# A layer norm's last pass split between VectorE and TensorE, and two background jobs moved in the order

## The chip, the core and the metric

The kernel runs on one core of a Trainium2 chip. The time is that of the device, in microseconds, from one execution; the figure of a kernel is the median of its runs. The profile is of one execution of its own.

A core has five engines, each with its own in-order queue: TensorE (PE in the profile, with its weight loads as PEld), VectorE (DVE), ScalarE (ACT), GpSimd (POOL) and SyncE (SP), which here only issues DMAs. An instruction that waits holds up what is queued behind it on its engine, and nothing else.

## The reference

One decoder layer over 512 tokens of width 2048, all in float32:

```
h   = x @ w_in                                   (11808 columns)
y_a = (FoX attention(q, k, v, forget gates) * silu(z)) @ w_a
y_b = (NSA attention(compressed, selected, window) * silu(z)) @ w_b
m   = sigmoid(g_a) * y_a + sigmoid(g_b) * y_b
out = layer_norm(2^(1/4) * x + m @ w_o, ln_g, ln_b)
```

The layer norm takes mean and variance over the 2048 columns of a token and gives `(z - mean) / sqrt(var + 1e-5) * g + b`. The NSA branch has a compression of keys and values: blocks of 32 tokens go through `gelu(flat @ w1) @ w2`.

## The kernel before, in words

**Splits.** Each f32 operand of a large product is split into a high part (`hi`, written by ACT as fp32r) and a rest (`lo`, written by DVE); a product is three fp32r matmuls, hi*hi, hi*lo and lo*hi (`mm3`, L106). Weights are streamed: a load into one of three buffers `wr` (L157, on SP's queue), a split into `wh` and `wl` (L97 on ACT, L98 on DVE) three units ahead of use, then the matmuls. A buffer `wr` is free for the next load when its last split is done.

**The stream and its ticks.** The program is one hand-written stream of units, most of them four k-tiles of a product. During a unit the code calls `tick()`, in the projections once per two k-tiles (6 matmuls). A tick advances every background job (a Python generator in the list `active`, in the order in which they were added, then the heads of two queues, `tq` and `sq`) to its next `yield`. So a yield is a step in the order of the program, not a wait of the chip: it sets between which matmuls an instruction stands in PE's queue, and between which splits it stands in DVE's. `drain` runs ticks until a condition holds.

**The background jobs that matter here.** When the first projection is done, `first_evac` starts three: a job with the forget gates (DVE steps L659 to L703, with a product at L679), `lefts` and `tables`.

- `lefts` (L1044) makes the left operands of four products of a Strassen-like scheme that follows (`phase_split`). It passes ten ticks, then issues one sum of two halves of x^T per tick (L1054, 16 of them, DVE), then one split per tick (16, ACT and DVE).
- `tables` loads rows of a one-hot table, makes two products with `rel` (L627), copies each out of PSUM with DVE (`tb`, L629), stores it, and then issues two transfers that spread the table in DRAM (`skew_d`, L632, 2560 KB, and `fwd_d`, L633). Its last PE step is a transposition at L635, which takes the one PSUM bank `m` that the second copy at L629 reads.
- `cmp_finish` (L799 on) ends the compression, once for keys and once for values: DVE copies the sums out of PSUM (`parts`, L805) and makes a matrix `two` (L806); two yields later PE multiplies them (L810); then follow the gelu and the second product, with yields between.
- `fox_s` and `fox_t` are the attention's two halves. `fox_s` normalizes the rows of `p` on DVE (L395, L399), `fox_t` transposes them on PE (L408).

**The last product.** `m @ w_o` is taken in four column blocks (n = 0 to 3) of 512. For n = 0 to 2 all four token tiles run together through 16 k-tiles, one tick per k-tile; afterwards `add_all` adds x with DVE (`add_z`, L1284) and takes the statistics of the block (L1285), one tile per tick. For n = 3 tiles 0 and 1 run first, while the split weights are kept; then `o_rest(2)` and `o_rest(3)` run tile 2 and tile 3 alone, 48 matmuls each, with seven ticks each. So the norm of tiles 0 and 1 is issued beside the matmuls of tiles 2 and 3, that of tile 2 beside tile 3 and after, and that of tile 3 at the end.

**The norm before.** `norm_job` adds the last block for its tiles, then goes through `norm_steps`: combine the statistics (L1296), root on ACT (L1297), reciprocal and shift on DVE (L1298, L1299). Of the four pieces of 512 columns, piece 1 is scaled on ACT (L1305) and gets g and b on POOL (L1306, L1307); the other three take two DVE passes each: `(z - mean) * g` (L1309) and `* rstd + b` (L1310). g and b are in SBUF, broadcast to all 128 partitions by DMAs that `f_open` starts at the beginning of the last product (`consts`, L1269). A piece is stored by SP's queue (L1313) when it is done.

Of the kernel before, what the change touches and what calls it, by code (L numbers as in the profile page):

```python
# [12 lines left out]
F32 = mybir.dt.float32  # L13
F32R = mybir.dt.float32r
AF = mybir.ActivationFunctionType
# [5 lines left out]
P = 128  # L21
# [42 lines left out]
def layer(ctx, tc, x, w_in, b_f, pos_k, pos_v, wk1, wk2, wv1, wv2, w_a, w_b, w_o, ln_g, ln_b, rel, onehot, out):  # L64
    nc = tc.nc

    def dram(t, off, ap):
        return bass.AP(tensor=t.tensor, offset=t.offset + off, ap=ap)
# [731 lines left out]
    def cmp_finish(kv):  # L800

        n = G * NCMP
        parts = small("parts", 2 * n, CMP_HID)
        two = small("two", 2 * n, n)
        nc.vector.tensor_copy(parts, hid[kv][:2 * n, :CMP_HID])  # L805
        nc.vector.tensor_tensor(two, ident[:2 * n, :n], ident[:2 * n, n:2 * n], op=ALU.add)  # L806
        yield
        yield
        m = bank("m", 1)
        nc.tensor.matmul(m[:n, :CMP_HID], two, parts, start=True, stop=True)  # L810
        a, u = small("ga", n, CMP_HID), small("gu", n, CMP_HID)
        nc.vector.tensor_copy(a, m[:n, :CMP_HID])
        yield
        nc.vector.tensor_tensor(u, a, a, op=ALU.mult)
        nc.vector.tensor_scalar(u, u, 0.044715, 1.0, op0=ALU.mult, op1=ALU.add)
        nc.vector.tensor_tensor(u, u, a, op=ALU.mult)
        yield
        nc.scalar.activation(u, u, AF.Tanh, scale=math.sqrt(2.0 / math.pi))
        yield
        nc.vector.tensor_scalar(a, a, 0.5, None, op0=ALU.mult)  # L820
        nc.vector.scalar_tensor_tensor(a, u, 1.0, a, op0=ALU.add, op1=ALU.mult)
        yield
        yield
        m = bank("m", 1)
        for k in range(2):
            nc.tensor.transpose(m[:, k * 64:k * 64 + n], a[:, k * P:(k + 1) * P], ident[:n, :n])
        mk = m[:, :P].rearrange("p (k c) -> p k c", k=2)[:, :, :n]
        if kv == "k":
            ht = small("ht", P, 2 * n).rearrange("p (k c) -> p k c", k=2)
            nc.vector.tensor_copy(ht, mk)  # L830
            yield
            yield
            m = bank("m", 1)
            for k in range(2):
                nc.tensor.matmul(m[:, :n], w2t[kv][:, k], ht[:, k], start=k == 0, stop=k == 1)
            for g in range(G):
                kc = pool("attn").tile([P, 2, CP], F32R, name=f"kc{g}")
                nc.vector.memset(kc[:, :, NCMP:].bitcast(F32), 0.0)
                split(kc[:, 0, :NCMP], kc[:, 1, :NCMP], m[:, g * NCMP:(g + 1) * NCMP])
                kt_["c", g] = kc  # L840
        else:

            ht = small("ht", P, 2 * G * C3).rearrange("p (k g u c) -> p k g u c", k=2, g=G, u=3)
            nc.vector.memset(ht, 0.0)
            for u in range(3):
                nc.vector.tensor_copy(ht[:, :, :, u, :NCMP], mk.rearrange("p k (g c) -> p k g c", g=G))
            yield
            yield
            m = bank("m", 1)
            for g in range(G):  # L850
                for k in range(2):
                    nc.tensor.matmul(m[:C3, g * P:(g + 1) * P], ht[:, k, g].rearrange("p u c -> p (u c)"),
                                     w2t[kv][:, k], start=k == 0, stop=k == 1)
            for g in range(G):
                vc = pool("attn").tile([C3, DH], F32R, name=f"vc{g}")
                vt["c", g] = vc
                src, low = m[:C3, g * P:(g + 1) * P], slice(2 * CP, C3)
                nc.scalar.activation(vc, src, AF.Copy)
                nc.vector.tensor_tensor(vc[low], src[low], vc[low].bitcast(F32), op=ALU.subtract)
        done.add(("cmp", kv))  # L860
        yield
        if kv == "v":
            active.append(block_bias())
# [179 lines left out]

    def lefts():  # L1044

        for _ in range(10):
            yield
        x32 = left["x"]
        t0, t1 = slice(0, S // 2), slice(S // 2, S)
# [203 lines left out]
    def f_open():  # L1253
        close_pool("o")
        fp = open_pool("fin")
        fin["res"] = fp.tile([P, 2, KR, S], F32R, name="res")
        fin["g"] = fp.tile([P, D], F32, name="lng")
        fin["b"] = fp.tile([P, D], F32, name="lnb")
        fin["eps"] = fp.tile([P, 1], F32, name="eps")
        nc.vector.memset(fin["eps"], EPS)  # L1260
        for i in range(NT):
            fin["st", i] = fp.tile([P, NC, 6], F32, name=f"st{i}")
            fin["mv", i] = fp.tile([P, 2], F32, name=f"mv{i}")
            fin["sd", i] = fp.tile([P, 3], F32, name=f"sd{i}")

        def consts():
            for c in range(NC):
                for t, src in (("g", ln_g), ("b", ln_b)):
                    nc.gpsimd.dma_start(fin[t][:, c * S:(c + 1) * S], dram(src, c * S, [[0, P], [1, S]]))  # L1269
                    for _ in range(4):  # L1270
                        yield
        active.append(consts())

    def load_z(n):
# [7 lines left out]
    def add_z(i, n, p):  # L1282
        z = fin["z", i, n]
        nc.vector.scalar_tensor_tensor(z, z, ALPHA, p, op0=ALU.mult, op1=ALU.add)  # L1284
        nc.vector.bn_stats(fin["st", i][:, n], z)  # L1285

    def add_all(n, banks):
        for i in range(NT):
            add_z(i, n, banks[i])
            yield  # L1290

    def norm_steps(i):
        mv, sd = fin["mv", i], fin["sd", i]

        def stats():
            nc.vector.bn_aggr(mv, fin["st", i])  # L1296
            nc.scalar.activation(sd[:, :1], mv[:, 1:2], AF.Sqrt, bias=fin["eps"])  # L1297
            nc.vector.reciprocal(sd[:, 1:2], sd[:, :1])  # L1298
            nc.vector.tensor_scalar(sd[:, 2:3], mv[:, :1], sd[:, 1:2], -1.0, op0=ALU.mult, op1=ALU.mult)  # L1299

        def piece(n):
            z, c = fin["z", i, n], slice(n * S, (n + 1) * S)
            g, b = fin["g"][:, c], fin["b"][:, c]
            if n == 1:
                nc.scalar.activation(z, z, AF.Identity, scale=sd[:, 1:2], bias=sd[:, 2:3])  # L1305
                nc.gpsimd.tensor_tensor(z, z, g, op=ALU.mult)  # L1306
                nc.gpsimd.tensor_tensor(z, z, b, op=ALU.add)  # L1307
            else:
                nc.vector.scalar_tensor_tensor(z, z, mv[:, :1], g, op0=ALU.subtract, op1=ALU.mult)  # L1309
                nc.vector.scalar_tensor_tensor(z, z, sd[:, 1:2], b, op0=ALU.mult, op1=ALU.add)  # L1310

        def store(n):
            nc.sync.dma_start(dram(out, i * P * D + n * S, [[D, P], [1, S]]), fin["z", i, n])  # L1313

        def steps():
            stats()
            yield
            piece(1)
            for n in (0, 2, 3):
                piece(n)  # L1320
                store(n)
                if n == 2:
                    store(1)
                yield

        return steps()

    def norm_job(tiles):
        for i, p in tiles:
# [169 lines left out]
```

## Time and profile before

| | us |
|---|---|
| runs shown | 1541.04, 1542.46, 1541.02 (median 1541.04) |
| the profiled execution | 1544.86 |
| its span, first to last instruction | 1542.8 |
| outside the span | 2.06 |
| mean granted clock of TensorE | 0.993 of full speed |

The page gives each engine's busy time and the chain of work that ended last: followed back from the last instruction, at each step to what released it. A group's row ends with its busy time, the mean of one in ns, and the idle time of the engine before it. In a timeline a row is start, length, engine, line of the code, operation, what it writes and reads, and in brackets the engine's idle time before it with what ended it. Matmuls are pipelined: the length of one is longer than the distance to the next. The clock is the share of full speed that the throttle granted TensorE.

### The profile page before, as it was taken

What the parts mean: (1) busy time and instruction counts of PE and PEld (TensorE: products, weight loads), DVE (VectorE), ACT (ScalarE), POOL (GpSimd) and SP (SyncE); (2) the same over time, 40 slices, a digit from 0 to 9 for tenths busy, and PEclk for the clock granted to TensorE, in tenths of its full rate; (3) what the DMA queues carried; (4) which work ended last, traced back from release to release, by engine and by line L of the source; (5) the groups of instructions that cost most, each with busy time, mean ns of one, the idle gap of its engine ahead of it and who ended that gap; (6) DMA issues with size and microseconds to landing.
All of it is one profiled execution on the core that took longest, in us unless ns stands there. A gap on an engine that the chain in (4) does not pass through costs nothing.

```text
span 1542.8 us, 19662 instructions
## 1 busy us (share of the span) xinstructions
PE 1503.5 (97%) x7143; PEld 1255.1 (81%) x7143; DVE 855.6 (55%) x1683; ACT 638.6 (41%) x1254; POOL 210.3 (14%) x333
## 2 busy tenths in 40 slices
PE   7999999999999999999999999999999999999995
PEld 5778787997897878888888888888888888888884
DVE  3857666666664664554445665366635444343347
ACT  6245555555563543433334444344434222222221
POOL 0102020211114632532000000000002000030003
PEclk9999999999999999999999999999999999999998
DMA  6578685877665553443333222322226343272222
GB/s 198 133 199 208 181 198 161 187 227 173 176 155 184 144 144 89 130 139 108 82 96 90 76 76 75 83 75 76 67 84 218 119 146 119 96 259 96 96 96 109
DMA packets 202241, 207.00 MB, mean 134 GB/s; under 512 B 12992, under 2 KB 153312, under 8 KB 202144
## 3 DMA queue, kind: packets, MB, share of 16 engines
q1 hardware_dynamic: 182288, 159.41, 34.8%
q0 software_dynamic: 19856, 46.34, 13.0%
q8 instruction: 56, 0.92, 0.2%
q14 instruction: 41, 0.34, 0.1%
HBM read 189.12 MB, written 20.22 MB: 136 GB/s over the span
## 4 chain that ended last, share of the span: by engine, by line
PE 87%; DVE 6%; DMA 3%; ACT 2%; issue 1%; POOL 0%; SPq 0%; ACTq 0%; DVEq 0%
PE d L106 48%; PE s L106 12%; PE pt L106 9%; PE o L106 8%; PE m L106 5%; DMA wr<-in_w_in_dram 2%; DVE wl L98 2%; PE pt L408 2%; ACT wh L97 1%; DVE om L1309 1%; PE m L112 1%; DVE om L1310 1%; PE o L112 0%; PE d L1219 0%; DVE c L977 0%
## 5 line engine op out<-in xcount | busy, mean ns | idle before, releaser
L106 PE MATMUL d<-big,wh 128*128 128x512 f32 x1792 | 570.4, 399 | 6.9 <-ACT wh L97 3.8
L98 DVE TENSOR_TENSOR wl<-wr,wh 128x512 fp32r<-128x512 f32 (+1 forms) x492 | 331.0, 681 | 379.7 <-ACT wh L97 369.8
L97 ACT ACTIVATE wh<-wr 128x512 fp32r<-128x512 f32 (+1 forms) x492 | 300.4, 619 | 394.2 <-PE d L106 126.4
L106 PEld LDWEIGHTS d<-big,wh 128*128 128x128 f32 x1792 | 325.3, 189 | 72.3 <-ACT wh L97 5.5
L106 PE MATMUL d<-big,wl 128*128 128x512 f32 x896 | 352.6, 394 | 0.1
L106 PEld LDWEIGHTS d<-big,wl 128*128 128x128 f32 x896 | 169.2, 189 | 38.4 <-DVE wl L98 0.9
L390 ACT ACTIVATE p<-p,mn 128x128 f32<-128x128 f32 (+3 forms) x96 | 54.1, 564 | 134.6 <-DVE mn L388 134.6
L98 DVE TENSOR_TENSOR wl<-s,wh 128x512 fp32r<-128x512 f32 (+1 forms) x120 | 75.2, 637 | 54.6 <-ACT wh L97 54.4
L97 ACT ACTIVATE wh<-s 128x512 fp32r<-128x512 f32 (+1 forms) x120 | 69.2, 589 | 58.6 <-DVE wl L98 32.6
L106 PE MATMUL s<-wh,T 128*128 128x512 f32 (+1 forms) x320 | 93.2, 367 | 0.0
L106 PE MATMUL o<-wh,big 128*128 128x512 f32 (+1 forms) x224 | 84.2, 376 | 2.7 <-ACT wh L97 2.7
L106 PE MATMUL m<-wh,big 128*128 128x512 f32 (+1 forms) x224 | 83.7, 374 | 0.0
L106 PE MATMUL d<-wh,big 128*128 128x512 f32 (+1 forms) x240 | 74.4, 376 | 0.0
L98 DVE TENSOR_TENSOR pT<-pt,pT 128x512 fp32r<-128x512 f32 (+1 forms) x96 | 46.6, 489 | 44.3 <-ACT pT L97 43.8
L789 POOL TENSOR_SCALAR af<-raw,posT 128x31 f32<-128x31 f32 x128 | 66.9, 545 | 0.1
L106 PEld LDWEIGHTS s<-wh,T 128*128 128x128 f32 x320 | 59.2, 188 | 7.5
L97 ACT ACTIVATE pT<-pt 128x512 fp32r<-128x512 f32 (+1 forms) x96 | 41.3, 433 | 47.4 <-PE pt L408 46.7
L106 PE MATMUL s<-wl,T 128*128 128x512 f32 (+1 forms) x160 | 58.7, 367 | 0.0
L951 POOL DMA_DIRECT2D r<-in_w_in_dram x20 | 24.2, 1209 | 199.4 <-DVE wl L98 118.6
L106 PEld LDWEIGHTS o<-wh,big 128*128 128x128 f32 x224 | 42.0, 188 | 10.6 <-ACT wh L97 4.6
L106 PEld LDWEIGHTS d<-wh,big 128*128 128x128 f32 x240 | 44.6, 188 | 7.2 <-ACT wh L97 0.4
L480 POOL DMA_DIRECT2D bt<-skew_d x8 | 4.3, 542 | 326.3 <-DVE mn L388 257.5
(276 smaller groups left out, 2400.4 us busy)
## 6 DMA issues: line engine op xcount, KB each, us to landing
wr<-in_w_in_dram SPq DMA_DIRECT2D x148, 512.0 KB, 3.7
wr<-in_w_o_dram SPq DMA_DIRECT2D x32, 512.0 KB, 3.6
wr<-in_w_in_dram SPq DMA_DIRECT2D x24, 384.0 KB, 3.8
wr<-in_w_a_dram SPq DMA_DIRECT2D x16, 512.0 KB, 3.6
om<-sig_d POOLq DMA_DIRECT2D x32, 256.0 KB, 4.8
wr<-in_w_b_dram SPq DMA_DIRECT2D x16, 512.0 KB, 3.7
r<-in_w_in_dram SPq DMA_DIRECT2D x12, 512.0 KB, 4.9
r<-in_w_in_dram POOLq DMA_DIRECT2D x12, 512.0 KB, 11.5
```

What stands on the lines that cost most here:

```text
L97: nc.scalar.activation(hi, src, AF.Copy)
L98: nc.vector.tensor_tensor(lo, src, hi.bitcast(F32), op=ALU.subtract)
L106: nc.tensor.matmul(o, u, v, start=first and n == 0, stop=last and n == 2, **kw)
L112: nc.tensor.matmul(*u, start=first and u is whole, stop=last and u is whole)
L390: nc.scalar.activation(row, row, AF.Exp, bias=it["mn"][:, i:i + 1], scale=-1.0, accum_out=it["l"][:, i:i + 1])
L408: nc.tensor.transpose(b[:, (i - j) * P:(i - j + 1) * P], pt[:, OFF[i] + j * P:OFF[i] + (j + 1) * P], ident)
L480: nc.gpsimd.dma_start(bt, dram(skew_d, h * P * RL + P - 1, [[RL - 1, P], [1, S]]))
L789: nc.gpsimd.tensor_scalar(af[:, l, g], src, posT[:, po0 + ll:po0 + ll + 1], None, op0=ALU.add)
L951: nc.gpsimd.dma_start(two(n, k), rows(jobs[j], quad[0] * kh + k - 1, quad[1]), accum_op=ALU.add)
L1309: nc.vector.scalar_tensor_tensor(z, z, mv[:, :1], g, op0=ALU.subtract, op1=ALU.mult)
L1310: nc.vector.scalar_tensor_tensor(z, z, sd[:, 1:2], b, op0=ALU.mult, op1=ALU.add)
```

## The change

Three edits.

The norm: after `add_all` has added a block for all tiles, four ticks later it multiplies each tile's block by g with DVE (`times_g`, one tile per tick); for the last block that product stands in `norm_steps`. What is then left of a piece is `z*g * rstd + (-mean*rstd * g + b)`. The bracket is made by PE in PSUM, as a product of two rows: the left operand is the column pair (-mean*rstd, 1) of `sd`, transposed by PE and copied to SBUF by ACT (`ct`, 2 x 128), the right one the rows g and b (`gb`, 2 x 2048, plain f32). One DVE pass per piece then reads the bank and is followed by the store. The steps of a tile are: statistics; transposition; pieces 0 and 1; pieces 2 and 3; each a tick apart. ACT's and POOL's work on piece 1 is gone, and so is the broadcast of b.

`lefts` passes four ticks instead of ten ahead of its first sum. `cmp_finish` passes four yields instead of two between its copies and the product.

```diff
         nc.vector.tensor_copy(parts, hid[kv][:2 * n, :CMP_HID])
         nc.vector.tensor_tensor(two, ident[:2 * n, :n], ident[:2 * n, n:2 * n], op=ALU.add)
-        yield
-        yield
+        for _ in range(4):
+            yield
         m = bank("m", 1)
...
     def lefts():
 
-        for _ in range(10):
+        for _ in range(4):
             yield
...
-        fin["b"] = fp.tile([P, D], F32, name="lnb")
+        fin["gb"] = fp.tile([2, D], F32, name="gb")
...
-            fin["sd", i] = fp.tile([P, 3], F32, name=f"sd{i}")
+            fin["sd", i] = fp.tile([P, 4], F32, name=f"sd{i}")
+            nc.vector.memset(fin["sd", i], 1.0)
+            fin["ct", i] = fp.tile([2, P], F32, name=f"ct{i}")
 
         def consts():
+            for r, src in enumerate((ln_g, ln_b)):
+                nc.gpsimd.dma_start(fin["gb"][r:r + 1], dram(src, 0, [[0, 1], [1, D]]))
             for c in range(NC):
-                for t, src in (("g", ln_g), ("b", ln_b)):
-                    nc.gpsimd.dma_start(fin[t][:, c * S:(c + 1) * S], dram(src, c * S, [[0, P], [1, S]]))
-                    for _ in range(4):
-                        yield
+                nc.gpsimd.dma_start(fin["g"][:, c * S:(c + 1) * S], dram(ln_g, c * S, [[0, P], [1, S]]))
+                for _ in range(4):
+                    yield
...
+    def times_g(i, n):
+        z = fin["z", i, n]
+        nc.vector.tensor_tensor(z, z, fin["g"][:, n * S:(n + 1) * S], op=ALU.mult)
+
     def add_all(n, banks):
         for i in range(NT):
             add_z(i, n, banks[i])
             yield
+        for _ in range(4):
+            yield
+        for i in range(NT):
+            times_g(i, n)
+            yield
 
     def norm_steps(i):
...
+        mv, sd, ct = fin["mv", i], fin["sd", i], fin["ct", i]
+        nc.vector.bn_aggr(mv, fin["st", i])
+        nc.scalar.activation(sd[:, 3:4], mv[:, 1:2], AF.Sqrt, bias=fin["eps"])
+        times_g(i, NC - 1)
+        nc.vector.reciprocal(sd[:, 2:3], sd[:, 3:4])
+        nc.vector.tensor_scalar(sd[:, :1], mv[:, :1], sd[:, 2:3], -1.0, op0=ALU.mult, op1=ALU.mult)
+        yield
+        m = bank("m", 1)
+        nc.tensor.transpose(m[:2, :P], sd[:, :2], ident)
+        nc.scalar.activation(ct, m[:2, :P], AF.Copy)
+        yield
+        for n in range(NC):
             z, c = fin["z", i, n], slice(n * S, (n + 1) * S)
...
+            b = bank(*(("pt", 2), ("pt", 2), ("o", 1))[n % 3])
+            nc.tensor.matmul(b, ct, fin["gb"][:, c], start=True, stop=True)
+            nc.vector.scalar_tensor_tensor(z, z, sd[:, 2:3], b, op0=ALU.mult, op1=ALU.add)
+            nc.sync.dma_start(dram(out, i * P * D + n * S, [[D, P], [1, S]]), z)
+            if n % 2:
                 yield
```

More of the change, by code (lines that the diff above doesn't have):

```diff
@@ L1290, in add_all @@
             yield
-    def norm_steps(i):
[L1293 to L1301, printed above, removed]
-            z, c = fin["z", i, n], slice(n * S, (n + 1) * S)
[L1303 to L1323, printed above, removed]
@@ L1324, in steps @@
                 yield
-        return steps()
     def norm_job(tiles):
```

## The prediction

> **What bounds the kernel now.** I read the page's head and its chain of work first, then busy time by stretches for the last 40 us, then the chain, the stretches and the timeline at the two other places that the change touches.
>
> ```profile
> span 1542.8 us, 19662 instructions
> ...
> PE 1503.5 (97%) x7143; PEld 1255.1 (81%) x7143; DVE 855.6 (55%) x1683; ACT 638.6 (41%) x1254; POOL 210.3 (14%) x333
> ...
> PE 87%; DVE 6%; DMA 3%; ACT 2%; issue 1%; POOL 0%; SPq 0%; ACTq 0%; DVEq 0%
> ```
>
> TensorE (PE) carries 87% of the chain: what is added to its stream is paid in full, and VectorE's (DVE's) work beside it is mostly covered. So I look for the places where PE does not set the time. The stretches of the tail (columns: stretch, length, busy time of PE, PEld, DVE, ACT and POOL, clock, DMA):
>
> ```profile
> 1502.30:1513.40 11.10, 11.10 (x50) 9.20 (x49) 10.13 (x17) 1.57 (x4) 3.27 (x2) 1.00 0.22 81
> 1513.40:1524.60 11.20, 11.20 (x50) 9.01 (x48) 10.62 (x14) 1.77 (x3) 5.12 (x4) 1.00 0.34 127
> 1524.60:1536.70 12.10, 0.09 (x1) 0.00 (x0) 11.40 (x15) 1.11 (x2) 4.65 (x3) 0.69 0.30 112
> 1536.70:1542.80 6.10, 0.00 (x0) 0.00 (x0) 0.00 (x0) 0.00 (x0) 0.00 (x0) 0.50 0.25 88
> ```
>
> From 1502.3 both engines are full: PE with the last column's tiles 2 and 3, DVE with the norm of tiles 0 and 1. PE stops at 1524.69; DVE goes on for 12 us, so the old norm is late by that much. The last 6 us are the last store and the program's end, the same in both kernels.
>
> The other places: the chain around 67 us, and stretches at both.
>
> ```profile
> 65.50 0.60 DVE x L1054
> ...
> 67.44 0.67 DVE wl L98
> ...
> 68.12 21.96 DMA wr<-in_w_in_dram
> ...
> 90.87 9.23 PE d L106 x31
> ```
>
> ```profile
> 566.90:570.30 3.40, 1.64 (x7) 1.04 (x7) 3.01 (x8) 0.81 (x2) 1.93 (x4) 0.95 0.41 120
> 570.30:573.70 3.40, 3.40 (x12) 2.74 (x11) 2.43 (x6) 1.90 (x4) 0.00 (x0) 0.54 0.68 224
> 89.04:92.45 3.41, 1.58 (x5) 1.03 (x6) 1.60 (x3) 2.26 (x5) 0.00 (x0) 0.95 0.82 250
> 92.45:95.90 3.45, 3.45 (x10) 2.65 (x10) 3.45 (x7) 3.45 (x8) 0.00 (x0) 0.55 0.46 115
> ```
>
> At 67 us DVE is the bound: it frees a weight buffer at 68.1, the load takes 22 us, and PE resumes at 90.87. At 567 us PE idles for 1.76 of 3.40 us. After both gaps the clock is at half for 3.4 us, which costs up to 1.7 us of PE work.
>
> **The change, part by part: the tail.** DVE loses one of two passes on three pieces of a tile, POOL both passes on the fourth. DVE gains one product with g per piece (three of four earlier, beside matmuls), and PE per tile one transposition and four plain f32 products of 2 rows by 512 columns.
>
> ```profile
> L1309 DVE SCALAR_TENSOR_TENSOR om<-om,mv,lng 128x512 f32<-128x512 f32 x12 | 13.0, 1085 | 0.0
> L1310 DVE SCALAR_TENSOR_TENSOR om<-om,sd,lnb 128x512 f32<-128x512 f32 x12 | 12.6, 1050 | 0.4
> ...
> L1208 DVE TENSOR_TENSOR om<-om 128x512 f32<-128x512 f32 x8 | 5.5, 692 | 0.3
> ```
>
> ```profile
> 50.39 1.02 PE L627 MATMUL m<-oh,rb 32*8 32x512 f32 x2
> 51.34 0.73 PE L106 MATMUL d<-big,wh 128*128 128x512 f32 x2
> ...
> 64.36 0.27 PE L635 MATMUL m<-ident,po 64*128 64x64 f32 x1 [0.67 <-DVE tb L629]
> 64.56 0.73 PE L106 MATMUL d<-big,wh 128*128 128x512 f32 x2
> ```
>
> ```profile
> 1481.17 21.09 PE d L106 x93
> ```
>
> DVE's 25.6 us in L1309 and L1310 become 16 passes of some 0.68 us (10.9) and, in the tail, 4 products of 0.69 (2.8). The other 12 products lie in stretches where PE carries the chain and the weights' splits run three steps ahead; with that cover gone they would cost 12 x 0.69 = 8.3 us.
>
> PE pays. No product of two rows exists before. The nearest is L627: plain f32, 512 moving columns, 32 rows; it shows as two records and holds PE from 50.39 to 51.34, 0.95 us. The other end is the kernel's own product (L106): 21.09/93 = 0.227 us. I take 0.96, by L627, since the new operands are plain f32 too. A transposition costs 0.20 (64.36 to 64.56), and I add 0.10 for its waiting check.
>
> Where these stand decides. The background steps run every second k-tile, 6 x 0.227 = 1.36 us apart, seven of them beside each of tiles 2 and 3. Tile 0 takes five; tile 1 reaches its transposition in the last step beside tile 2; its products and all of tile 2's fall beside tile 3. So 12 products and 3 transpositions stand in PE's queue ahead of tile 3's last matmul: 12 x 0.96 + 3 x 0.30 = 12.4 us. One wait comes with them: tile 2's transposition is issued 1.36 us after tile 1's last product, but DVE then has a last pass, statistics, the g product and two small steps to do, some 2.2 us. Tile 3's matmuls, queued behind it, stand still for 0.8 us. PE's end moves by 13.2, to 1537.9.
>
> Then the last tile alone, in the old timeline:
>
> ```profile
> 1527.93 0.68 DVE L1284 SCALAR_TENSOR_TENSOR om<-om,s 128x512 f32<-128x512 f32 x1
> 1528.65 0.69 DVE L1285 BATCH_NORM_STATS2 st<-om 128x6 f32<-128x512 f32 x1
> 1529.38 0.26 DVE L1296 BATCH_NORM_AGGREGATE mv<-st 128x2 f32<-128x24 f32 x1
> 1529.68 0.29 ACT L1297 ACTIVATE sd<-mv,eps 128x1 f32<-128x1 f32 x1 [7.07 <-DVE mv L1296]
> 1530.00 0.16 DVE L1298 RECIPROCAL sd<-sd 128x1 f32<-128x1 f32 x1 [0.36 <-ACT sd L1297]
> 1530.20 0.21 DVE L1299 TENSOR_SCALAR sd<-mv,sd 128x1 f32<-128x1 f32 x1
> ...
> 1535.89 0.75 DVE L1310 SCALAR_TENSOR_TENSOR om<-om,sd,lnb 128x512 f32<-128x512 f32 x1
> ```
>
> ```profile
> 584.43 0.20 ACT L97 ACTIVATE kc<-m 128x31 fp32r<-128x31 f32 x1 [4.11 <-PE m L835]
> ```
>
> Sum and statistics 0.70 + 0.68 + 0.27; the g product 0.64 (it covers the root); reciprocal and shift 0.41; transposition and copy 0.6 (the copy by L97's 0.20); four products 3.84, with the passes behind them and only the last one showing, 0.9 with its latency. That is 8.0 us, against 1536.64 - 1524.69 = 11.95 before. **Tail: 13.2 + 8.0 - 11.95 = +9.2 us.** By the ends of the product's price: +0.7 at 0.227, +11 at 1.03. PE idles for 2.8 us ahead of the last products, longer than the 1.76 us at 567, so I expect the half clock there; 3.4 us of it cost 1.7, the 2.2 us that the products fill at least 1.1, **+1.3**.
>
> Here a rule of the Trainium skill differs from the rows (TensorE: Matmul & The Clock Gate, What's actually happening): it lets the clock fall to half after a whole idle window of about 3.4 us. This trace shows the fall after stretches that were 46 and 48% busy. By the page's rule neither the new gap nor the one at 567 us would have to pay; that case is a rival below.
>
> **The sums of x^T.** Six steps earlier puts six more sums on DVE ahead of the buffer that the chain shows.
>
> ```profile
> 49.28 0.42 DVE L686 TENSOR_SCALAR fs<-fe 8x512 f32<-8x512 f32 x1 [0.70 <-ACT fe L684]
> ...
> 53.67 0.69 DVE L295 SCALAR_TENSOR_TENSOR zo<-zo,d 128x512 f32<-128x512 f32 x1 [0.20 <-ACT zo L294]
> ...
> 63.63 0.67 DVE L629 COPY tb<-m 8x512 f32<-8x512 f32 x1
> ```
>
> ```profile
> 65.22 1.13 POOL L632 DMA_DIRECT2D skew_d<-rel_d  x1
> ```
>
> A sum takes 0.60 us in the chain, so 3.6; the idle times of 0.70 and 0.20 take in 0.9. DVE is then 2.7 late and, a link of the chain, has no gap up to 68. So the table's copy (L629) comes at 66.3; PE, which waited 0.67 us for it at L635, waits 3.3; the table's spread (L632) and the weight load start 2.7 later, and PE resumes at 93.5 instead of 90.87: +2.7. Bounds: 0, if DVE's gaps took all, and 3.6; below nothing only by the rival on this load. The long wait at L635 pulls the half clock forward, into time that PE would spend waiting for the load anyway; the wait at the load shrinks to about 1.2 us and brings none: -1.7. **+1.0.** The splits of T that come earlier gain nothing: after 92.45 PE is busy throughout.
>
> **The compress step's added yields** (two more before L810).
>
> ```profile
> 568.72 0.61 PE L810 MATMUL m<-parts,two 124*62 124x256 f32 x2 [1.76 <-DVE r L395]
> ```
>
> ```profile
> 568.68 0.49 DVE L399 TENSOR_SCALAR p<-p,r 128x512 f32<-128x512 f32 x1
> ```
>
> L810 no longer stands ahead in PE's queue while DVE is late: 1.76 us go. Late next is the transposition at L408, one step on, which needs the row that L399 ends at 569.17; PE would be there at 566.96 + 1.36 = 568.3. So 0.9 of the gap stays, and the half clock goes (1.7). **-2.5**, between -0.9 (no fall of the clock to save) and -3.5 (nothing late next).
>
> The rest I cost at nothing: the memsets and the loads of g and b (two rows and one broadcast in place of two broadcasts) are issued at the start of the last product, columns ahead of their use; on POOL's queue only the loads of x stand behind them, due a column later. The weights' splits on DVE behind the g products have three steps of slack.
>
> **Sum:** 9.2 + 1.3 + 1.0 - 2.5 = +9.0 us. The profiled execution took 1544.86 us, its span 1542.8 and 2.06 around it: 1553.9 by its own time. The median of the runs shown is 3.8 lower, perhaps without the half clocks; I carry the difference over: **1550.0 us**. A difference under about 0.2% (3.1 us) can't be told from none here.
>
> **Rivals.**
> A, the cheap product: if two rows cost PE one pass, 0.227, the tail is +0.7 without a fall of the clock, and 0.7 + 1.0 - 2.5 = -0.8: 1540.2, not slower. The tail changes by 13 us per us of price, so it decides below 0.52 us a product (+3.1 in sum). L627's 0.95 speaks against it; that its rows are 32, not 2, leaves it open. Faster by 0.2% it is only with -3.5 at 567 us and nothing lost at 68.
> B, the load at 68 us no longer late: started against other traffic, the 22 us shrink and PE's gap before 90.87 (2.9 us) and its half clock go: -4.6 in place of +1.0, so +3.4: 1544.4. Against it: the table's spread and the load move together, both behind DVE.
> C, the clock neither falls in the tail nor was saved at 567 and 90: 9.2 + 2.7 - 0.9 = +11.0: 1552.0. The two half clocks in the trace speak against it; the lower median speaks for it.
> D, PE's queue waits: each transposition comes before DVE is done, with tiles 1 and 2 losing 1.5 to 2 us more: +13: 1554. DVE's free time between passes speaks against it.
>
> **How the numbers follow.** Forecast 0.54, C 0.18, D 0.10, B 0.08 (half of it within 0.2%), A 0.10 (0.04 of it faster, 0.06 within). Faster 0.04, same 0.10, slower 0.86. The range takes in B, C and the price of 1.03 and leaves out A and the far side of D: 1544.0 to 1554.5.
>
> **What would show it.** Right: two records per new product, 0.9 to 1.0 us from start to start; PE's last matmul of tile 3 some 13 us later; DVE idle between passes in the tail; the wait at L635 above 2 us; PE resuming near 93; no gap at L810, a smaller one at L408. Wrong: products at a quarter of a microsecond, or a first weight load that lands earlier than before.

## The result, and the profile after

| | before | after |
|---|---|---|
| runs, us | 1540.0 to 1542.46, median 1541.03 (4 runs) | 1554.35, 1560.1, 1563.44, 1561.65; median 1560.88 |
| ratio of after to before | | 1.0122, 95% interval 1.0089 to 1.0154 |
| the profiled execution | 1544.86 | 1554.35 |
| its span | 1542.8 | 1552.5 |
| mean granted clock of the four runs after, in their order | | 0.995, 0.989, 0.988, 0.988 |

The changed kernel is slower by 19.85 us; 9.0 were forecast, and the range ended at 1554.5. The profiled execution of the changed kernel is the fastest of its four runs and took 9.49 us more than the profiled execution of before. So there are two things to explain: 9.5 us that the profiles show, and some 6 to 9 more that the other three runs have, at a lower mean clock.

The head of the page after, with the shares of the chain of work that ended last:

```profile
span 1552.5 us, 19741 instructions
...
PE 1524.1 (98%) x7179; PEld 1259.2 (81%) x7179; DVE 851.8 (55%) x1695; ACT 634.9 (41%) x1254; POOL 193.7 (12%) x323
...
PE 89%; DVE 5%; DMA 3%; ACT 2%; issue 1%; POOL 0%; SPq 0%; ACTq 0%; DVEq 0%
```

PE's busy time grew by 20.6 us. DVE's fell by only 3.8, because the passes that went are paid back in part by the products with g. Busy time went from the engine that carried 6% of the chain to the one that carried 87% of it.

The stretches after (columns as before: stretch, length, busy time of PE, PEld, DVE, ACT and POOL, clock, DMA):

```profile
68.86:72.27 3.41, 3.41 (x10) 2.63 (x10) 3.19 (x8) 1.12 (x2) 0.95 (x2) 0.55 0.56 105
...
89.04:92.45 3.41, 3.34 (x15) 2.44 (x13) 0.00 (x0) 0.09 (x1) 0.00 (x0) 1.00 0.92 266
...
566.90:570.30 3.40, 3.40 (x16) 2.78 (x16) 1.96 (x6) 1.86 (x4) 2.23 (x5) 1.00 0.58 157
...
1502.30:1513.40 11.10, 11.10 (x40) 6.77 (x39) 5.38 (x11) 0.57 (x2) 0.00 (x0) 1.00 0.13 49
...
1536.59:1540.00 3.41, 0.88 (x4) 0.38 (x3) 2.38 (x6) 0.29 (x1) 0.00 (x0) 0.95 0.00 0
1540.00:1549.00 9.00, 7.56 (x9) 2.58 (x9) 3.08 (x5) 0.27 (x1) 0.00 (x0) 0.50 0.23 87
1549.00:1552.50 3.50, 0.00 (x0) 0.00 (x0) 0.00 (x0) 0.00 (x0) 0.00 (x0) 0.50 0.19 75
```

The gap at 567 us is gone, and PE is nearly full in the stretch ahead of 92. In the tail DVE, which was busy for 10.13 of 11.10 us from 1502.3 on, is now busy for 5.38, while PE, full as before, gets through 40 records in place of 50. The last rows hold a surprise: from 1540 to 1549 PE is busy for 7.56 of 9.00 us, in the last tile's products, and its clock stays at half all the way. (The edges of the stretches in this text lie some 0.3 us behind the changes of the clock, hence the 0.95 to 0.97 of a stretch with a fall at its end; times of a change are given by the clock itself.)

The chain of waits after, at the products beside tile 2 (start, length, what; x4 are the four records of two products):

```profile
1507.56 1.91 PE pt L1320 x4
1509.47 1.59 PE s L106 x6
1511.06 1.05 PE o L1320 x2
1512.11 0.86 PE pt L1320 x2
```

Two records per product, and four products take 1.91 + 1.05 + 0.86 = 3.82 us: 0.955 each, all of it on the chain. The timeline after, for the end:

```profile
1526.08 0.27 PE L1314 MATMUL m<-ident,sd 128*2 128x128 f32 x1 [0.27 <-DVE sd L1311]
...
1537.08 0.39 PE L106 MATMUL s<-wh,big 128*128 128x512 f32 x1
...
1540.87 3.78 PE L1320 MATMUL pt<-gb,ct 2*128 2x512 f32 x4 [0.36 <-ACT ct L1315]
...
1544.44 1.91 PE L1320 MATMUL o<-gb,ct 2*128 2x512 f32 x2
...
1546.15 1.91 PE L1320 MATMUL pt<-gb,ct 2*128 2x512 f32 x2
...
1548.10 0.75 DVE L1321 SCALAR_TENSOR_TENSOR om<-om,sd,pt 128x512 f32<-128x512 f32 x1 [0.96 <-PE pt L1320]
```

PE's last matmul of tile 3 ends at 1537.47, where it was 1524.69. The last four products start at 1540.87 and come 1.7 to 1.8 us apart, twice the distance of those above, and each pass of DVE waits 0.96 us for its product. DVE ends at 1548.85, and the span 3.65 us later; before, it was 1536.64 and 6.16. That difference of 2.5 us shows in the queue's own waits of SP, first in the kernel before and then in the one after (waiting queue, what it waited for: us in total, times, the longest):

```profile
SPq L1494 <- PEq L1494: 3.1, 2, 2.6
```

```profile
SPq L1492 <- PEq L1492: 0.7, 2, 0.5
```

PE's queue is only the last link of that wait. At the program's end each engine's queue has a `DRAIN` behind its last work, and then the queues signal one another. POOL's instructions there, before and then after (count, shortest, median and longest in ns, first and last start in us):

```profile
L1494 POOLq EVENT_SEMAPHORE  x4: 17/17/17, 1542.1 to 1542.7; - x4
L1494 POOLq DRAIN  x3: 46/93/9028, 1533.0 to 1542.6; - x3
```

```profile
L1492 POOLq DRAIN  x3: 46/98/8924, 1370.1 to 1552.2; - x3
```

Before, POOL's first `DRAIN` is issued with POOL's last product, at 1533.0, and lasts 9.03 us, to 1542.1; POOL's next step is at 1542.1, the other queues' follow it, and the span ends 0.7 us behind it. DVE had been done since 1536.64, and SP's wait for the last store ended 3.8 us ahead of the span's end. After, POOL has no piece of the norm: its `DRAIN` of 8.92 us lies at 1370, and SP's wait for the last store ends 1.3 us ahead of the end. So the end of the old program hung on POOL, not on DVE and the store.

### The profile page after: what moved, and what is told of

The parts are those of the page before. It is cut to its first block, busy times and chain, and to the rows that moved or that the text cites. A ratio compares the mean times of both kernels' runs of the same rounds, so it can differ in the third digit from the quotient of the medians.

```text
span 1552.5 us, 19741 instructions
## 1 busy us (share of the span) xinstructions
PE 1524.1 (98%) x7179; PEld 1259.2 (81%) x7179; DVE 851.8 (55%) x1695; ACT 634.9 (41%) x1254; POOL 193.7 (12%) x323
## 4 chain that ended last, share of the span: by engine, by line
PE 89%; DVE 5%; DMA 3%; ACT 2%; issue 1%; POOL 0%; SPq 0%; ACTq 0%; DVEq 0%
PE d L106 47%; PE s L106 13%; PE pt L106 9%; PE o L106 9%; PE m L106 6%; DMA wr<-in_w_in_dram 2%; DVE wl L98 2%; PE pt L408 2%; ACT wh L97 1%; PE pt L1320 1%; PE m L112 1%; PE o L112 0%; PE d L1219 0%; PE o L1320 0%; DVE x L1054 0%
## 5 line engine op out<-in xcount | busy, mean ns | idle before, releaser
L106 PEld LDWEIGHTS m<-wh,big 128*128 128x128 f32 x224 | 42.1, 188 | 6.4
```

The lines of the kernel that those rows point to most:

```text
L106: nc.tensor.matmul(o, u, v, start=first and n == 0, stop=last and n == 2, **kw)
```

## The experiments

The theory: the loss is the norm's, and lies in two places, the price of the products on a full PE, and a clock that these products let fall, by luck in some runs more than in others. The rivals: the two moved jobs cost something too; the loss is in waits in PE's queue, not in the products; the products are dear for their time alone and the clock falls for other reasons. Each ratio below is against the kernel before on the same chip, whose medians were 1539.98 to 1541.72 us over the four sets of runs.

### e1_norm_only and e2_lefts_cmp: which edit costs

The changed kernel with `lefts` and `cmp_finish` as before, and the kernel before with those two edits alone.

```diff
 # e1_norm_only, against the changed kernel; e2_lefts_cmp is the reverse, against before
-        for _ in range(4):
-            yield
+        yield
+        yield
...
-        for _ in range(4):
+        for _ in range(10):
```

> The norm edit alone; lefts and cmp_finish as before. Theory H (the two-row products count as idle for TensorE's clock, so in most runs the clock falls to half several times between 1502 and 1537 us, up to 1.7 us each): median 1555 to 1561 us, runs several us apart, the slower ones with a mean clock near 0.988. Rival F (the extra of the unprofiled runs comes from the front of the kernel, where lefts makes VectorE late): 1549 to 1552 us (1541 + 9.2 + 1.3), runs within 2 us of one another.

> The two moved jobs alone; the norm as before. Theory H: 1541 to 1545 us (+2.7 for the sums, -0.9 to -2.5 for the yields, a half clock more or less), runs within 3 us. Rival F: 1548 us or more, with runs several us apart.

Measured: the norm alone 1559.52 us (6 runs, 1555.09 to 1566.2), ratio 1.012 [1.0099, 1.0141], mean clocks 0.985 to 0.991. The two moves alone 1541.64 us (12 runs), 1.0008 [0.9998, 1.0018]. The norm carries the whole loss, and the moves together are worth nothing that can be measured.

The stretches of the first show what the profile of the changed kernel didn't hold:

```profile
1505.05:1508.46 3.41, 3.41 (x11) 1.61 (x10) 1.49 (x2) 0.00 (x0) 0.00 (x0) 0.96 0.01 5
1508.46:1511.87 3.41, 3.41 (x7) 1.62 (x6) 0.00 (x0) 0.00 (x0) 0.00 (x0) 0.50 0.42 154
1511.87:1515.29 3.42, 3.42 (x7) 1.63 (x6) 2.33 (x6) 0.29 (x1) 0.00 (x0) 0.50 0.20 78
1515.29:1518.70 3.41, 3.41 (x11) 2.49 (x10) 0.16 (x1) 0.00 (x0) 0.00 (x0) 0.54 0.19 75
1518.70:1522.11 3.41, 3.41 (x15) 2.42 (x14) 0.00 (x0) 0.27 (x1) 0.00 (x0) 1.00 0.00 0
```

And its chain, in the same place:

```profile
1505.68 1.91 PE pt L1320 x4
...
1509.92 2.00 PE o L1320 x2
1511.92 1.71 PE pt L1320 x2
```

PE is busy for all of these 17 us, and yet the clock falls to half at 1508.2, right after a stretch of which one pair of two-row products fills 1.91 us. At half clock the next pair takes 3.71 instead of 1.91 and reaches into two stretches, and the clock comes back only after 10.24 us. From tile 2's start to PE's last matmul it is 40.39 us here, against 35.64 in the changed kernel's profile, which has no such fall: 4.75 us lost. So a full PE isn't enough to hold the clock; in this trace a stretch with these products can be followed by the fall that elsewhere follows idle time. The Trainium skill (TensorE: Matmul & The Clock Gate, What's actually happening) has the clock go by whether PE is active in windows of about 3.4 us. The 3.41 us between the changes of the clock here agree; that PE is busy throughout and is slowed all the same does not.

### e3_rows128 and e8_rows32: the same products over more rows

If it is the number of rows, the same product with rows of zeros added must hold the clock at the same price. The left operand is `sdp`, padded with zero columns before it is transposed, and `gb` gets zero rows.

```diff
-        fin["gb"] = fp.tile([2, D], F32, name="gb")
+        fin["gb"] = fp.tile([P, D], F32, name="gb")
+        nc.vector.memset(fin["gb"], 0.0)
+        fin["sdp"] = fp.tile([P, P], F32, name="sdp")
+        nc.vector.memset(fin["sdp"], 0.0)
+        nc.vector.memset(fin["sdp"][:, 1:2], 1.0)
...
-        nc.tensor.transpose(m[:2, :P], sd[:, :2], ident)
-        nc.scalar.activation(ct, m[:2, :P], AF.Copy)
+        nc.tensor.transpose(m[:, :P], sdp, ident)
+        nc.scalar.activation(ct, m[:, :P], AF.Copy)
```

(e8_rows32: 32 rows in place of 128.)

> The changed kernel with the shift product taken over 128 rows, 126 of them zero, in place of 2: the same number of products, columns and passes. Theory H, with the clock going by the rows a product uses: no fall of the clock between 1502 us and the end of tile 3's matmuls in any run, runs within 3 us, median 1550 to 1555 us, mean clock 0.994 or more. If the clock goes by something else in these products (plain f32, their length, the waits around them), or the extra lies at the front: as the changed kernel, 1554 to 1563 us.

> The shift product over 32 rows, 30 of them zero, between the changed kernel's 2 (1554 to 1566 us) and 128 (1547.7 to 1551.4 us). If TensorE's clock goes by the share of rows in use, a quarter of the rows leaves half clocks between 1502 us and the end of tile 3's matmuls: 1552 to 1560 us, runs some us apart. If a block of 32 rows is enough to count as busy: 1548 to 1552 us, mean clock 0.996 or more.

Measured: 128 rows 1549.91 us (6 runs, 1547.7 to 1551.41), 1.0057 [1.0043, 1.0071], mean clocks 0.996 to 0.999; 32 rows 1552.09 us (4 runs), 1.0068 [1.0054, 1.0081], clocks 0.995 and 0.996. Both lie below the changed kernel's interval. The stretch with twelve of the products, in the run over 128 rows, and then that run's timeline at the end:

```profile
1500.00:1536.00 36.00, 34.37 (x130) 23.55 (x128) 16.98 (x32) 1.72 (x6) 0.00 (x0) 1.00 0.23 88
```

```profile
1538.21 3.68 PE L1324 MATMUL pt<-gb,ct 128*128 128x512 f32 x4 [0.37 <-ACT ct L1319]
...
1541.73 1.02 PE L1324 MATMUL o<-gb,ct 128*128 128x512 f32 x2
...
1542.59 1.02 PE L1324 MATMUL pt<-gb,ct 128*128 128x512 f32 x2
```

The first pair of the last tile is slow as in the changed kernel, behind the same idle wait. Then the clock comes back and the next two take 0.86 from start to start, where the two-row products stayed at 1.7.

Not all that e3 gains is the clock. Beside the kernel's own matmuls a pair over 128 rows is also cheaper than one over 2. Two rows of e3's timeline, with one pair between them:

```profile
1518.65 1.95 PE L106 MATMUL s<-res,big 128*128 128x512 f32 x6
...
1521.75 1.96 PE L106 MATMUL s<-res,big 128*128 128x512 f32 x6
```

Six matmuls and a pair take 3.10 us here; in the changed kernel's chain above it was 1.59 + 1.05 + 0.86 = 3.50, at full clock too. From tile 2's start to PE's last matmul it is 33.56 us in e3's profile, against 35.64: 2.1 us that aren't the clock. Why the rows matter here isn't shown. The 32 rows have no such gain, 3.50 and 35.66 us, so e8 is the cleaner test of the clock: the same work at the same price, no fall from 1502 us to the end of tile 3's matmuls in its profile, and by the two ratios (1.0122 and 1.0068) 0.54% or some 8 us less. What is left of the loss in e8, 0.68%, is in the main the time on a full PE, less what the shorter work of DVE and the shorter end of the program save. In e3 0.65% or some 10 us went, of which 2.1 are the cheaper pairs. Its 1549.9 us is the forecast's 1550.0 by coincidence: neither those pairs nor the shorter end of the program was in the forecast.

Since all added rows hold zeros, it is not their data. Over 32 rows the clock holds beside the matmuls, but in the one profile it doesn't come back in the last tile.

### e4_four_at_once: all products of a tile in one step

```diff
-            if n % 2:
-                yield
+        yield
```

> The changed kernel with all four products of a tile in one step, 3.9 us of two-row products in a row instead of two pairs. Theory H: a stretch of 3.4 us can no longer miss them, so the profile itself shows a half clock behind the products of each of tiles 0 to 2, and every run has at least three falls there; 1554 to 1562 us. Rival F: full clock in the profile from 1502 us to the end of tile 3's matmuls.

Measured: 1553.15 us (4 runs, 1551.95 to 1555.09), 1.008 [1.0063, 1.0098]. The median is below what was expected, and 7.7 us below that of the changed kernel, though the two intervals touch. Its stretches at tiles 0 and 1:

```profile
1505.13:1508.54 3.41, 3.41 (x8) 1.14 (x7) 2.24 (x3) 0.00 (x0) 0.00 (x0) 0.97 0.20 79
1508.54:1511.96 3.42, 3.42 (x9) 2.69 (x9) 1.75 (x5) 0.29 (x1) 0.00 (x0) 0.53 0.59 228
1511.96:1515.37 3.41, 3.41 (x14) 2.17 (x13) 0.00 (x0) 0.27 (x1) 0.00 (x0) 1.00 0.02 5
1515.37:1518.78 3.41, 3.41 (x10) 1.43 (x9) 2.79 (x4) 0.00 (x0) 0.00 (x0) 0.97 0.39 152
1518.78:1522.20 3.42, 3.42 (x10) 2.73 (x9) 1.62 (x4) 0.00 (x0) 0.00 (x0) 0.53 0.40 155
```

A group of four fills nearly a stretch, and behind those of tiles 0 and 1 the clock falls, but for one stretch only, in which the kernel's own matmuls stand. Behind tile 2's group it stays at 1.00, so the three falls expected were two: that group lay across two stretches, with 1.97 us of products in the first. Pairs are better spread by the eye and worse by the clock: at half clock each pair takes 3.7 us and keeps the clock down for the pair behind it. Whether a first pair makes it fall differs from run to run. The Trainium skill (TensorE: Matmul & The Clock Gate, What's actually happening) calls the windows free-running, so that a kernel's work falls into them otherwise in each execution. The changes of the clock in the changed kernel's profile agree that they keep a beat of their own: from 71.96 to 1539.69 us it is 430 times 3.413. That this is the whole reason isn't shown. Nor is it shown how much of a stretch the products must fill. Two stretches, cut here by the clock's own beat, first of e1 and then of e4, with the products alone (columns: stretch, length, busy time of PE and PEld, clock, DMA; the last product's overlap counts in):

```profile
1504.74:1508.16 3.42, 1.98 (x4) 0.66 (x4) 1.00 0.00 0
```

```profile
1525.42:1528.84 3.42, 1.97 (x5) 1.00 (x6) 1.00 0.00 0
```

The products fill the same time in both, yet the clock fell behind the first and stayed at 1.00 behind the second.

### e11_one_pass: the product at a quarter of the price

```diff
-        fin["gb"] = fp.tile([2, D], F32, name="gb")
+        fin["gb"] = fp.tile([2, D], F32R, name="gb")
...
-            fin["ct", i] = fp.tile([2, P], F32, name=f"ct{i}")
+            fin["ct", i] = fp.tile([2, P], F32R, name=f"ct{i}")
```

g and b are loaded into two rows of the buffer of g first and copied into `gb` by ACT, which rounds them.

> The changed kernel with the shift product in fp32r, one pass; it leaves out the low parts of the shift, of g and of b in that product. Two rows, as changed. If the price of the plain f32 product is the main term: products of 0.23 us in the profile and, since a pair now fills under 0.5 us of 3.4, no half clock before the end of tile 3's matmuls: 1541 to 1546 us, runs within 4 us. Rival: the norm's cost lies in its waits and its order (transposition, VectorE behind PE) more than in the product's price: 1548 us or more.

Measured: 1540.92 us (11 runs, 1540.09 to 1542.59), 1.0002 [0.9993, 1.0011]. Its timeline:

```profile
1524.52 0.50 PE L1326 MATMUL o<-gb,ct 2*128 2x512 f32 x1
1524.85 0.39 PE L1326 MATMUL pt<-gb,ct 2*128 2x512 f32 x1
```

One record a product, 0.33 us from start to start, and no half clock from 70.2 to 1534.5 us. Both parts of the loss are gone together, and the whole change then comes out at no difference: DVE's shorter tail and the shorter end of the program are worth what the transpositions, their waits and the cheap products cost. It doesn't tell the price from the clock, since it takes away both; e8 and e3 do that.

### e5_cmp_only, e6_lefts_only, e7_later_sums, e9_sums13: the moved jobs

```diff
 # e5_cmp_only against before: cmp_finish with four yields, lefts as before
-        yield
-        yield
+        for _ in range(4):
+            yield
 # e6_lefts_only against before: lefts with 4 ticks, cmp_finish as before
-        for _ in range(10):
+        for _ in range(4):
 # e7_later_sums, e9_sums13: as e5, with 16 and 13 ticks in lefts
```

> The two added yields of cmp_finish alone. By the prediction's terms: 1.76 us of PE's gap go, 0.6 to 0.9 come back as a wait of the transposition L408 for L399, and where the gap had brought the half clock 1.7 go too: -0.9 to -2.5 us, 1538.2 to 1539.8 us. Rival: the gap is hidden by a later wait, no difference, 1540.7 us within 1.

> The sums of x^T six ticks earlier, alone. By the prediction's terms: VectorE 2.7 us later at the weight buffer freed near 68 us, so +2.7 us, less 1.7 where the half clock moves into the wait at L635: +1.0 to +2.7 us, 1541.7 to 1543.4 us. Rival: VectorE's gaps take the sums in, no difference, 1540.7 us within 1.

> The opposite of the change's second edit: lefts passes 16 ticks, not 10 or 4, with cmp_finish as changed and the norm as before. If VectorE's queue is what sets the weight load near 68 us, six sums of 0.6 us fewer ahead of it bring the load 3 to 3.6 us forward: PE's gap of 2.9 us before 90.87 and the half clock behind it go: with the yields' -0.9 to -2.5, 1534 to 1538 us. Rival: the six splits of T that now come late, issued together when the next product opens, cost what was gained: 1539 to 1542 us.

> lefts passes 13 ticks; cmp_finish as changed; norm as before. Three sums fewer ahead of the weight buffer (1.8 us): PE's gap of 2.9 us before 90.87 shrinks to about 1.1 and brings no half clock; three splits of T come late when the next product opens (1.4 us each, half of what cost 2.8 us with 16 ticks), inside the three units of slack. So 1.8 to 3.5 us under the yields alone (0.9983 of before): about 0.996 of before, 1535 to 1537 us. Rival: late splits cost what is gained, 0.998 or more.

| | median, us (runs) | ratio |
|---|---|---|
| yields alone (e5) | 1538.3 (11) | 0.9983 [0.9973, 0.9993] |
| sums at the fourth step alone (e6) | 1545.32 (9) | 1.0021 [1.0012, 1.0031] |
| yields, sums at the 16th (e7) | 1541.7 (12) | 0.9998 [0.9989, 1.0007] |
| yields, sums at the 13th (e9) | 1538.35 (12) | 0.998 [0.9971, 0.9988] |

By the ratios, of some 1541 us, the yields gain 2.6 us and the early sums lose 3.2, more than the 1.0 to 2.7 expected. If sums before the late buffer are bad, later ones should be good; 1534 to 1538 us were expected of e7, and it took 1541.7. PE's waits from 60 to 120 us, in e5, e7 and e9 in this order (engine, line, what it waited for: us, times, longest):

```profile
PE d L106 <- ACT wh L97: 2.5, 1, 2.5
```

```profile
PE pt L106 <- ACT wh L97: 2.8, 1, 2.8
```

```profile
PE pt L106 <- ACT wh L97: 0.9, 1, 0.9
...
PE pt L106 <- DVE wl L98: 0.3, 1, 0.3
```

The wait for the weights near 90 us (2.5) goes in e7, and one of 2.8 comes at 111 to 114 us, with the clock at half for 6.83 us behind it, where the products of the split sums begin and the splits, now late, alternate between ACT and DVE. At 16 ticks the order of these sums moves the gap, it doesn't take it away. At 13 ticks both waits are small, but 12 runs give no more than e5; the 0.996 expected was a miss, and where the gain of the profile went isn't shown.

### e10_last_tile and e12_all_on_dve: is there a version that gains?

e10 is e9 with two DVE passes on all four pieces of tiles 0 to 2 and the new scheme for the last tile only. e12 is e9 with two DVE passes on every piece of every tile, nothing on ACT or POOL, and three small transpositions on PE behind the last tile's pieces, whose results nobody reads.

```diff
 # e12_all_on_dve, against before, with e9's two edits
-            if n == 1:
-                nc.scalar.activation(z, z, AF.Identity, scale=sd[:, 1:2], bias=sd[:, 2:3])
-                nc.gpsimd.tensor_tensor(z, z, g, op=ALU.mult)
-                nc.gpsimd.tensor_tensor(z, z, b, op=ALU.add)
-            else:
-                nc.vector.scalar_tensor_tensor(z, z, mv[:, :1], g, op0=ALU.subtract, op1=ALU.mult)
-                nc.vector.scalar_tensor_tensor(z, z, sd[:, 1:2], b, op0=ALU.mult, op1=ALU.add)
+            nc.vector.scalar_tensor_tensor(z, z, mv[:, :1], g, op0=ALU.subtract, op1=ALU.mult)
+            nc.vector.scalar_tensor_tensor(z, z, sd[:, 1:2], b, op0=ALU.mult, op1=ALU.add)
...
-            piece(1)
-            for n in (0, 2, 3):
+            for n in range(NC):
...
+                if i == NT - 1 and n < NC - 1:
+                    nc.tensor.transpose(bank("m", 1)[:, :P], fin["z", i, n][:, :P], ident)
```

> As e9, and a norm mixed from both kernels: tiles 0 to 2 take two VectorE passes on all four pieces (nothing on POOL or ACT), only the last tile takes the two-row products, when PE has no matmuls left to delay. VectorE's work for three tiles is 3 x 7.9 = 23.6 us, so it ends 1 us behind PE's end; then 8.0 us for the last tile in place of 11.95 behind PE's end, with the half clock of the last products 1.3 more: 1 to 3 us under e9, 1533 to 1535.5 us. Rival: the products at half clock (1.7 us each, as in the changed kernel's last tile) take the gain back: as e9 within 1 us.

> As e9, with no shift product at all: all four pieces of every tile take two VectorE passes, POOL and ACT none, and on PE three small transpositions whose results nobody reads follow the last tile's first pieces. VectorE: 7.9 us a tile by the last-tile run's rows, 31.6 for four, against 34.35 with POOL's passes beside it, so -2.7 us. The end of the program: SyncE waits 2.6 us for PE's sequencer where PE had been idle for over 10 us and 0.5 where it had just worked; if idleness is the cause, another -2.1 us. Together about 1533 to 1534 us, 0.995 of before. Rivals: without the 2.1 (the wait has another cause) 1535 to 1536; VectorE's passes not shorter without POOL beside them, 1538.

Measured: e10 1535.89 us (5 runs), 0.9963 [0.9951, 0.9975]; e12 1532.6 us (5 runs, 1531.71 to 1533.58), 0.9951 [0.9937, 0.9965], the fastest of all. In e10's profile the last four products are at half clock again (3.78 for the first two, 1.91 for each of the others), and from DVE's first sum of the last column block to its end it is 35.0 us against 34.4 before; the gain is at the program's end, 3.64 us from DVE's end instead of 6.19 in e9, since POOL's last `DRAIN` lies at 1488 us. So the 2.6 us that e10 has on e9 by the ratios, within the 1 to 3 expected, came from another place than expected. In e12 both things gain. DVE's timeline in e9 and then in e12:

```profile
1525.03 1.75 DVE L1309 SCALAR_TENSOR_TENSOR om<-om,mv,lng 128x512 f32<-128x512 f32 x1
1526.82 1.63 DVE L1310 SCALAR_TENSOR_TENSOR om<-om,sd,lnb 128x512 f32<-128x512 f32 x1
```

```profile
1514.57 0.75 DVE L1303 SCALAR_TENSOR_TENSOR om<-om,mv,lng 128x512 f32<-128x512 f32 x1
1515.35 0.75 DVE L1304 SCALAR_TENSOR_TENSOR om<-om,sd,lnb 128x512 f32<-128x512 f32 x1
```

With POOL at work on its piece, one pair of DVE's passes in a tile takes 3.4 us; without POOL every pass takes 0.75, so that the fourth piece costs DVE 1.5 us and saves it 1.9. POOL's piece was no relief. The Trainium skill (SBUF — State Buffer, SBUF: two separate sides) has a pair of ports that GpSimd shares with a DVE instruction of two SBUF inputs, and that one of them holds for a whole instruction. These rows agree: POOL's own passes last 1.58 to 1.66 us, and a DVE pass beside them grows to about that. From PE's last matmul to DVE's end it is 9.3 us in e12's profile against 11.9 in e9's, and the end of the program 3.7 against 6.2: 5.1 of the 5.5 us between their spans (1530.6 and 1536.1). By the ratios, from two sets of runs, e12 is 4.5 us ahead of e9. The end of the program shrank as expected, but the traces give another reason than PE's idleness. In all six kernels with POOL in the norm a `DRAIN` of POOL of 9.03 or 9.04 us is over 0.8 us ahead of the span's end, and that end comes 6.2 us after DVE's; in the eight without, that `DRAIN` is over 39 us or more ahead of the end, which then comes 3.6 to 3.9 us after DVE's. No run leaves POOL out and PE idle, so that the three transpositions do anything isn't shown.

## Why the prediction was wrong, point by point

**The sum of the profiled execution held.** From the two profiles: tile 2 starts 0.9 us earlier (1501.83 against 1502.77), PE's last matmul ends 35.64 us after that instead of 21.92 (+13.7), from there to DVE's end it is 11.4 instead of 11.95 (-0.6), and the end of the program is 2.5 shorter: +9.7 of span, +9.49 of own time, for a forecast of +9.0. Its terms held less well, as the next points show.

**PE's end**: 13.2 forecast, 13.7 measured. From start to start a product took 0.955 for the 0.96 taken, but the kernel's matmuls beside a pair are slower too: six matmuls and a pair take 3.50 us, six matmuls alone 1.36, so that a pair holds PE for 2.14 and the six pairs for 12.8, not 11.5. The transpositions and their waits make up for most of it: 0.9 is left for them, against 0.9 + 0.8 forecast; the wait at tile 2's was 0.27, and the 0.10 added to each for a waiting check stood on no row (the first two, which wait for nothing, push the matmuls behind them back by 0.12 in all). The ends given for the tail, +0.7 at 0.227 and +11 at 1.03, don't follow from the prediction's own 13 us per us of price, which from +9.2 gives -0.3 and +10.1.

**The last tile**: 8.0 and 1.3 for the half clock forecast, 11.4 measured. The term for the half clock was too small: it was counted for one stretch of 3.4 us, of which the products would fill 2.2, and lasted through all four products, which take 7.0 us at half clock (3.57 for the first two, 1.71 for each of the others) where 3.84 was counted.

**The last 6 us, "the same in both kernels"**: wrong by 2.5, in the other direction. The old end hung on POOL's `DRAIN`, which takes 9.03 us from POOL's last product on; taking POOL out of the norm takes it off the end. That row was in the profile before, and wasn't read. This miss and the last tile's cancel within 0.4 us, so the sum looks better than its terms.

**The sums and the yields**: -1.5 forecast for both in the profile, -0.9 measured; but one profile each can't settle it, since e1, with neither edit, starts tile 2 at 1499.95, 2.8 us earlier than before. The waits after, from PE's side:

```profile
PE m L635 <- DVE tb L629: 3.2, 1, 3.2
PE d L106 <- ACT wh L97: 0.7, 1, 0.7
...
PE pt L408 <- DVE p L399: 0.6, 1, 0.6
```

3.3 us were forecast at L635, 1.2 where PE resumes and 0.9 at L408. PE resumes at 93.04 (93.5 forecast), with no half clock there, and one at 68.55 instead. By the ratios of e5, e6 and e2, the yields are worth -2.6 (-2.5 forecast), the sums +3.2 (+1.0 forecast), and both together +1.2 with an interval from -0.3 to +2.8.

**The step that failed** is "I carry the difference over", together with the term for the half clock, +1.3. It takes one execution's difference for the median's, and it counts the half clock in the last tile alone. The sum treated the twelve products beside tiles 2 and 3 as PE work like any other: that the clock could fall there was put at nothing, without a reason. The runs showed that it does fall there in some executions, 10.24 us at half clock and 4.75 us lost in e1's profile, and the profiled execution of the changed kernel was the one of four that was spared. The three others ran at a mean clock of 0.988 or 0.989, not 0.995. A difference of 0.006 or 0.007 over 1,558 us is 19 to 22 us at half clock, half of it lost where PE is full: 9 to 11 us as an estimate from these clocks, against 5.8 to 9.1 measured. That the clock is the difference is what e8 shows: the same products over 32 rows, at the same price, and some 8 us gone.

**The rule of the Trainium skill** was weighed as a reason for fewer falls of the clock, and the rows as the reason for more. The rows were right, and went further than the text took them: the clock fell behind a stretch that was 100% busy, too. (By the clock's own changes, at 92.12 and 569.99, the two stretches of before were 37 and 48% busy: 1.25 and 1.65 of 3.41 us.)

**The rivals**: A (cheap product) was refuted by two records a product; e11 comes out at 1540.9 with the cheaper product, near A's 1540.2, but partly by the shorter end of the program, which A didn't have. B didn't happen: the load took 21.10 us, issued at 71.15. C, the clock, had the right subject and the wrong sign: it supposed that fewer falls would matter than the forecast took. D, the waits in PE's queue: the wait at tile 2's transposition came to 0.27 us in the profile, and at tiles 0 and 1 there was none.

## What to carry to other kernels

A product of few rows isn't a small product: its columns and its passes are paid in full on an engine that sets the end, and it doesn't hold TensorE's clock. Where an edit changes what TensorE does in a stretch, compare the mean clock of several runs before a single profile's difference is taken for the kernel's. Look at what an "idle" engine does to its neighbours before work is taken off it or given to it: here POOL's help slowed DVE by more than it saved, and POOL's `DRAIN` held up the end of the program. Where a trace puts a wait down to an engine that has long been idle, look for what that engine itself waited for.

## What the hardware showed that was not expected

- The clock went by rows in use. Plain f32 products of 2 rows let it fall with PE 100% busy and did not bring it back (half clock from 1539.7 to the end); 128 rows, 126 of them zeros, held it, and brought it back after one stretch. 32 rows held it beside full matmuls, and in the one profile did not bring it back in the last tile. Where between 2 and 32 the border lies was not tried.
- The fall is a matter of luck in part: the same program ran at mean clocks from 0.985 to 0.991 in six executions, 1555.09 to 1566.2 us.
- Beside matmuls over 128 rows a pair of plain f32 products takes 2.14 us over 2 or 32 rows and 1.74 over 128 (six matmuls and a pair 3.50 and 3.10, less 1.36). Why isn't shown.
- POOL's `DRAIN` at the program's end takes 9.03 us from POOL's last product, 7.4 of them after that product's end (1534.65, against 1542.06). Where POOL's last work lies near the end it sets the end of the program: 6.2 us after DVE's in six kernels with POOL in the norm, 3.6 to 3.9 in eight without.
- A DVE pass of 0.75 us took 1.63 to 1.78 us while POOL worked on a piece of its own.
